# Low parts of the attention keys on both halves of the partitions, in a hybrid two-layer trunk

## The chip, the cores and the metric

The kernel runs on one core of a Trainium2 chip. The metric is the device time of one execution in microseconds (us), lower being better. Before the change the median of 3 runs is 1223.11 us (1218.67 to 1227.75). A difference of about 1% is what a measurement of this kernel can tell from no change.

The engines go by short names: PE is the matrix engine (PEld its weight loads, which overlap with matmuls), DVE the vector engine, ACT the scalar engine, POOL the GpSimd engine, and SP the queue that issues most loads from DRAM. Matmuls read their two operands from SBUF, a memory of 128 partitions, and write to PSUM, eight banks of 128 x 512 floats.

## What is computed

A decoder trunk of two layers on 512 tokens of 1024 columns, in float32. Layer 0 mixes with a sliding-window attention (mixer A: 8 heads over 2 key heads, window 128) and a forgetting attention (mixer B: 8 heads, each with its own keys). Layer 1 mixes with a sparse attention (mixer C: 8 heads over one key head, the 128 best keys of each query by an indexer of 4 heads) and a latent attention (mixer D: 8 heads). Each layer ends in a mixture of 16 experts, of which every token takes two. Cut to what matters here:

```python
logits = jnp.einsum('bqhd,bshd->bhqs', q_i, k, preferred_element_type=jnp.float32) * scale
logits = logits + c_i[..., :, None] - cum[:, :, None, :]          # mixer B
p = jax.nn.softmax(jnp.where(pos[None, :] <= t[:, None], logits, -jnp.inf), axis=-1)
dots = jnp.einsum('bqhe,bse->bqhs', qi_i, k_idx, preferred_element_type=jnp.float32) * IDX_DIM ** -0.5
score = jnp.einsum('bqh,bqhs->bqs', w_i, jax.nn.relu(dots))       # indexer of mixer C
_, idx = lax.top_k(score, top_k)
```

The head dimension is 64 in A, B, C and the indexer. Mixer D has 96 and isn't touched by the change.

## The kernel before, in words

**Numbers in two parts.** A value that enters an important matmul is split into a high part H with 12 significant bits and a low part L, the rest. A projection takes three matmuls (`mm3`, lines 196 to 199: H by H, H by L, L by H), each with 128 partitions of each operand. The splits stand in `unit` (line 176, weights: H by ACT on line 184, L by DVE or POOL on line 185) and `split_to` (line 201).

**Heads.** A projection gives two heads at once, one on partitions 0 to 63 and one on 64 to 127 (`HALF`, line 298). `stack_q` (line 305) makes for each head one tile of 128 partitions: the head's qH on its own half and its qL on the other. `stack_k` (line 313) makes for each key head a tile with kH on both halves (`dup`: ACT writes the head's own half on line 317, POOL copies it to the other half on line 303) and puts kL of both heads in one tile, each on its own half (`low`: DVE, line 319). Then `logits` (line 322) takes two matmuls into one PSUM bank:

```python
T.matmul(Sp, q, dup, start=True, stop=False)
T.matmul(Sp, q[HALF[h]], low[HALF[h]], start=False, stop=not more)
```

The first (line 324) has 128 rows and gives qH kH + qL kH; the second (line 325) has 64 rows, those of the head's own half, and adds qH kL.

**Where logits are called.** `attn_a` (line 710; 4 pairs of heads x 4 tiles of 128 queries x 2 heads = 32 calls, 128 or 256 keys wide), `attn_b` (line 748; 32 calls, 128 to 512 keys; a bf16 matmul that adds the mask follows, line 385), `index_scores` (line 915; 12 calls, 256 to 512 keys) and `attn_c` (line 1003; 32 calls, 128 to 512 keys). That makes 108 calls. A softmax follows, for two heads together (line 335): a maximum on DVE (line 344 where a bias is added, else line 348), an exponential on ACT (line 358), a division on DVE (line 366). Then come transposes on PE (line 374), a copy to SBUF on ACT (line 377) and the product with the values on PE (line 380, which writes 64 columns of the array at a time).

**Order of the work.** Instructions are issued in an order that a scheduler makes from the program's own order and its model of costs; it puts projections between the logits and the later steps of attention, so that PE has work while a softmax runs. The order of each engine is fixed when the program is built. The even mixer (layer 0, from line 618) runs the values, A's keys, then q and attention of A in turns, then k and q of B's first four heads (`k_b(0)`, `q_b(0)`), their attention, `k_b(1)`, `q_b(1)`, and their attention by tile of queries, with the output projection between (`EVEN_ORDER`). The odd mixer (from line 833) runs the latents, the keys `kc` of C and `ki` of the indexer (line 901 to 906), the indexer's scores, and then the parts named in `ODD_ORDER`: attention D beside `top_keys` (line 967, DVE: 16 rounds of maximum and replacement for each of three tiles), then attention C. `kc` and `ki` already have both H and L on both halves: lines 905 and 906 split both parts and copy both to the other half.

**Memory.** In the even mixer keys lie in two slots `ks0` and `ks1` of 6 x 512 floats a partition (`k_tiles`, line 640: four `dup` and two `low`). A's keys take ks0, `k_b(0)` ks1, `k_b(1)` ks0 again. The experts' pool `mo` lies over the mixer's memory once that is done: a place for the first loads of weights (`AHEAD`, line 42) is written when what the mixer kept there has been read. SP issues these loads in a fixed order.

Of the kernel before, what the change touches and what calls it, by code (L numbers as in the profile page):

```python
# [9 lines left out]
F32 = mybir.dt.float32  # L10
# [23 lines left out]
# slots of an expert for its tokens; with more than these, dense_moe  # L34
CAP = 96
OOB = 2048.0
# banks for products of long sums, of short ones, transposes and the branches' outputs
PS_A, PS_S, PS_T, PS_O = 2, 3, 2, 1
# loads of experts' weights in the ring of their own
RING = 5  # L40
# the loads that are issued while the mixer runs, in order: numbers in the order of their use
AHEAD = (2, 3, 4, 0, 1, 5, 6, 8, 9, 10, 12, 13, 7, 14, 11, 15)
# columns on DVE, the others on Pool and ScalarE: of the affine part of a layer's first LN, by tile; of the last step of
# its second. Columns on Pool: of that LN's centring
# [3 lines left out]
# units whose low parts Pool brings, not DVE: (matrix, expert) -> numbers  # L48
LOW_ON_POOL = {("d", 14): (3,), ("d", 15): (2,)}
# orders of the parts that may be moved against each other: what they are stands where they are run  # L50
# [15 lines left out]
def trunk_kernel(ctx: ExitStack, tc, x_in, even_w_in, even_b_f, even_sinks, odd_w_in,  # L66
# [12 lines left out]
    class Rows:  # L79
        """[8 * 128, S] in two tiles"""  # L80
# [20 lines left out]
    # key - query, in the last blocks of a row of keys  # L101
# [11 lines left out]
    # the activations' table, ahead of the first use  # L113
# [14 lines left out]
    # heads' slopes and their inverses are powers of two: 2^-(h+1)  # L128
# [5 lines left out]
    # slots, counted from one  # L134
# [7 lines left out]
    # tokens, less 2048  # L142
# [8 lines left out]
    def spread(dst, src):  # L151
        """a row to all partitions, which costs DRAM but one of them"""
        nc.gpsimd.dma_start(dst[0:1, :], src.unsqueeze(0))
        G.partition_broadcast(dst, dst[0:1, :], channels=128)
# [21 lines left out]
    def unit(w, eng=V):  # L176
        """w = H + L with 12 significant bits each; w: [128, a, b], at most 1024 elements"""
# [10 lines left out]
    def ksplit(w, n, eng=V):  # L188
        """units along k: list over k of (H, L) rows"""
# [15 lines left out]
    def rsqrt(var, eps, n, pin=lambda ins: ins):  # L205
        """1 / sqrt(var + eps): first bits from the exponent, then a step of third order and one of second"""
# [3 lines left out]
        def square(r, v):  # L210
            """r * r * v"""
# [13 lines left out]
        # q * (15 - 10 c + 3 c c) / 8 without its factor 3/8, which the last step brings  # L225
# [7 lines left out]
    def ln_stats(sts):  # L233
        """-> means and variances [128, n, 2], 1/sqrt(var + eps) [128, n]"""
        n = len(sts)
        mv = sm.tile([128, n, 2], F32, name="mv", tag=f"mv{n}")
        for j, st in enumerate(sts):
            V.bn_aggr(mv[:, j, :], st)
        return mv, rsqrt(mv[:, :, 1], LN_EPS, n)
# [10 lines left out]
    def affine(x, gb, bb, nv):  # L250
        """x * gb + bb, the last nv columns on DVE"""
# [5 lines left out]
    # residual stream, updated in place  # L257
    xr = [None] * NT

    def new_xr(j, nm="xr"):  # L260
        """room for two tiles of it"""
# [17 lines left out]
    def proj_t(w, XH, XL, eng=V):  # L279
        """[128 columns, tokens] = w^T x; w: raw view [128, 8, 128]"""  # L280
# [15 lines left out]
    # heads in pairs, on 64 partitions each; logits as [qH; qL] . [kH; kH] + qH . kL, a pair's other head with  # L296
    # qL above qH
# [7 lines left out]
    def stack_q(o, scales, dst):  # L305
        """o: a pair's queries [128, S] -> dst: one tile for each head"""
# [6 lines left out]
    def stack_k(o, dup, low):  # L313
        """o: keys of two heads [128, S] -> dup: [kH; kH] for each head, low: kL of both"""
        for h in range(2):
            a, b = HALF[h], HALF[1 - h]
            A.copy(dup[h][a], o[a])
            ins = copy_pool(dup[h][b], dup[h][a])
            V.tensor_tensor(out=low[a], in0=o[a], in1=dup[h][a].bitcast(F32), op=ALU.subtract)
        return ins  # L320

    def logits(Sp, h, q, dup, low, more=False):
        """q: [128, queries], dup and low: [128, keys]"""
        T.matmul(Sp, q, dup, start=True, stop=False)
        T.matmul(Sp, q[HALF[h]], low[HALF[h]], start=False, stop=not more)

    def pair(n, get):
        """two heads' [128, n], side by side in one tile where they fit, and what to copy to have both"""
# [6 lines left out]
    def softmax(work, Sp, n, bias=None, slopes=None, sink=None, norm=V):  # L335
        """two heads' logits in PSUM -> probabilities in SBUF. bias: a [128, n] tile for each head, or None.
        slopes: (list of two slopes, their negatives [128, 2]): the logits come divided by the slope.
        sink: (sinks over slopes [128, 2], sinks [128, 2])"""
# [44 lines left out]
    def causal(S_, nb):  # L383
        """adds the mask to the diagonal block, the last of nb"""
        T.matmul(S_[:, (nb - 1) * 128:nb * 128], idb, trib, start=False, stop=True)

# [8 lines left out]
    def router_fold(l):  # L395
        """the router on x1 = (y - mean) * rstd * g + b, from y and rstd alone: the weights times g, less their
        mean over the rows, and b's part"""
# [15 lines left out]
    def choose(t0, t1):  # L413
        """fills O and M for some tiles from aff: one-hot choices, their sum"""
# [5 lines left out]
        # the two best of four add up to the largest sum of a pair  # L420
# [9 lines left out]
        # the first of the best groups; the others sink  # L430
# [25 lines left out]
    def weights():  # L456
        """the choices' affinities over their sum"""
# [9 lines left out]
    def slots(sl, oh0, t0, t1):  # L467
        """slots of some tiles' tokens, counted from one: of each expert, 0 elsewhere; the first expert's one-hot"""
# [3 lines left out]
        # a tile's tokens come after those of all tiles before  # L472
# [930 lines left out]
```

## Time and profile before

| | |
|---|---|
| median of 3 runs | 1223.11 us |
| the runs | 1218.67, 1227.75, 1223.11 us |
| span of the profiled execution, first to last instruction | 1213.8 us |
| what lies around the span, against the median | 9.3 us |
| first matmul of the logits, A | 48 us |
| last logits of B | 203 us |
| first matmul of the experts, layer 0 | 284.8 us |
| indexer's logits | 646 to 663 us |
| logits of C | 755 to 828 us |
| mean granted clock of PE | 0.955 |

The profile gives no time of its own for the profiled execution beside its span; the runs' times are of other executions. How to read it: the view by stretches gives the busy time of each engine in a stretch, with the number of its instructions in brackets. A matmul's end is modelled and neighbours overlap, so a busy PE says that PE had something in flight, not that it ran at its peak. What a matmul really costs in a row of matmuls is the distance from its start to the next one's start, which the timeline shows. A form such as `64*128 64x256` is a matmul with 64 rows by 128 columns of weights, and 256 columns streamed past. The granted clock is the share of the full rate at which PE was let run.

### The profile page before, as it was taken

Reading aid. Unit: us, or ns where it says so; the run is one execution under the profiler, and the core shown is the slowest. Engines: PE = TensorE matmul, PEld = TensorE weight load, DVE = VectorE, ACT = ScalarE, POOL = GpSimd, SP = SyncE. Lnnn points to the kernel's source line nnn. Section 1 sums busy time; section 2 is a strip of 40 time slices with the busy share of each in tenths; the row PEclk is TensorE's granted clock in tenths of the full one; section 3 lists DMA queues with packets and bytes.
Section 4 is the critical chain, followed back from the end, with each engine's and each line's share of the span. In section 5 each row is a group of like instructions: output and inputs, shape, how many; then the busy total and the mean of one; then the engine's idle time right before and its main releaser. Section 6 shows DMA issues by size and latency. Waiting matters only on the chain. (4 is left out here: it accounts for less than half of the span.)

```text
span 1213.8 us, 16654 instructions
## 1 busy us (share of the span) xinstructions
PE 1128.6 (93%) x5739; PEld 823.3 (68%) x5739; DVE 939.1 (77%) x1866; ACT 763.0 (63%) x1229; POOL 263.4 (22%) x223
## 2 busy tenths in 40 slices
PE   6999999988999999998599999999889999999982
PEld 6786776876777777776377665677767777777761
DVE  3646546587999999996866999455879999999967
ACT  3447455234888888886335745444348888888862
POOL 2001230052111141103602234001421111411023
PEclk9999999998999999999699999699889999999986
DMA  8313423488999997997412211222789999979962
GB/s 203 114 35 67 92 53 140 165 315 298 309 344 354 346 342 252 362 368 244 136 27 70 70 35 63 77 105 93 263 315 302 341 354 350 333 250 359 376 209 111
DMA packets 139613, 262.25 MB, mean 216 GB/s; under 512 B 11831, under 2 KB 28247, under 8 KB 139520
## 3 DMA queue, kind: packets, MB, share of 16 engines
q1 hardware_dynamic: 129232, 234.62, 55.9%
q0 software_dynamic: 10288, 26.48, 8.8%
q8 instruction: 47, 0.77, 0.3%
q14 instruction: 46, 0.38, 0.1%
HBM read 246.73 MB, written 22.30 MB: 222 GB/s over the span
## 5 line engine op out<-in xcount | busy, mean ns | idle before, releaser
L185 DVE TENSOR_TENSOR wl<-wraw,wh 128x1024 fp32r<-128x1024 f32 (+1 forms) x418 | 504.3, 1232 | 83.6 <-ACT wh L184 73.8
L184 ACT CAST wh<-wraw 128x1024 fp32r<-128x1024 f32 (+3 forms) x436 | 445.4, 1038 | 149.0 <-PE ps_s L199 66.3
L197 PE MATMUL ps_s<-wh,m 128*96 128x512 f32 (+1 forms) x528 | 208.7, 395 | 1.7 <-ACT m L202 1.7
L198 PE MATMUL ps_s<-wl,m 128*96 128x512 f32 (+1 forms) x528 | 206.8, 392 | 0.0
L199 PE MATMUL ps_s<-wh,m 128*96 128x512 f32 (+1 forms) x528 | 205.2, 389 | 0.4 <-DVE m L203 0.4
L199 PEld LDWEIGHTS ps_s<-wh,m 128*96 128x96 f32 x528 | 86.7, 164 | 35.7 <-DVE m L203 1.3
L197 PEld LDWEIGHTS ps_s<-wh,m 128*96 128x96 f32 x528 | 86.9, 165 | 34.5 <-ACT m L202 2.1
L198 PEld LDWEIGHTS ps_s<-wl,m 128*96 128x96 f32 x528 | 86.7, 164 | 31.9
L198 PE MATMUL ps_a<-wl,hH 128*96 128x512 f32 x256 | 101.7, 397 | 5.6 <-POOL wl L185 5.6
L197 PE MATMUL ps_a<-wh,hH 128*96 128x512 f32 x256 | 102.8, 402 | 3.4 <-ACT hH L202 3.4
L199 PE MATMUL ps_a<-wh,hL 128*96 128x512 f32 x256 | 101.1, 395 | 1.3 <-DVE hL L203 1.3
L197 PE MATMUL ps_a<-wh,XH 128*128 128x512 f32 (+2 forms) x224 | 88.4, 395 | 2.4 <-ACT wh L184 1.3
L1096 POOL DMA_INDIRECT m<-x1d,idx x30 | 33.2, 1106 | 255.1 <-PE ps_t L1107 233.9
L199 PE MATMUL ps_a<-wh,XL 128*128 128x512 f32 (+2 forms) x224 | 87.7, 391 | 0.4 <-DVE XL L203 0.4
L1171 POOL DMA_INDIRECT yd<-m,idx x30 | 49.0, 1634 | 177.1 <-ACT m L1170 176.1
L198 PE MATMUL ps_a<-wl,XH 128*128 128x512 f32 (+2 forms) x224 | 86.8, 388 | 0.0
L377 ACT COPY pT<-ps_t 128x512 f32<-128x512 f32 (+2 forms) x88 | 43.7, 519 | 52.8 <-PE ps_t L374 49.7
L198 PE MATMUL ps_a<-XL,wh 128*128 128x512 f32 x160 | 65.9, 412 | 0.0
L197 PE MATMUL ps_a<-XH,wh 128*128 128x512 f32 x160 | 65.5, 410 | 0.0
L199 PE MATMUL ps_a<-XH,wl 128*128 128x512 f32 x160 | 65.1, 407 | 0.3 <-DVE wl L185 0.3
L358 ACT ACTIVATE p<-p,nm 128x256 f32<-128x256 f32 (+3 forms) x96 | 50.7, 530 | 19.4 <-DVE nm L351 11.6
L198 PEld LDWEIGHTS ps_a<-wl,hH 128*96 128x96 f32 x256 | 41.5, 162 | 22.1 <-POOL wl L185 7.0
(325 smaller groups left out, 1934.7 us busy)
## 6 DMA issues: line engine op xcount, KB each, us to landing
wraw<-in_moe_w_up_dram SPq DMA_DIRECT2D x64, 1024.0 KB, 11.6
wraw<-in_moe_w_gate_dram SPq DMA_DIRECT2D x64, 1024.0 KB, 12.0
wraw<-in_moe_w_down_dram SPq DMA_DIRECT2D x64, 1024.0 KB, 11.9
wraw<-in_w_o_dram SPq DMA_DIRECT2D x6, 1024.0 KB, 4.9
wraw<-in_even_w_in_dram SPq DMA_DIRECT2D x4, 1024.0 KB, 5.1
x1d<-xr POOLq DMA_DIRECT2D x8, 512.0 KB, 7.6
yd<-xr POOLq DMA_DIRECT2D x8, 512.0 KB, 9.3
xr<-yd SPq DMA_DIRECT2D x8, 512.0 KB, 5.1
```

What stands on the lines that cost most here:

```text
L184: first(A.copy(hv, w))
L185: first(eng.tensor_tensor(out=lv, in0=w, in1=hv.bitcast(F32), op=ALU.subtract))
L197: T.matmul(o, lh, rh, start=first, stop=False)
L198: T.matmul(o, lh, rl, start=False, stop=False)
L199: T.matmul(o, ll, rh, start=False, stop=last)
L358: A.activation(out=pt[h], in_=(pt if bias else Sp)[h], func=AF.Exp, bias=nm[:, h:h + 1], scale=(slopes[0][h] if slopes else 1.0), accum_ou ...
L377: A.copy(d_, s_)
L1096: G.indirect_dma_start(out=xg_of[e], out_offset=None, in_=x1d[:, :], in_offset=bass.IndirectOffsetOnAxis(ap=idx[:CAP, e:e + 1], axis=0), b ...
L1171: G.indirect_dma_start(out=yd[:, :], out_offset=bass.IndirectOffsetOnAxis(ap=idx[:CAP, e:e + 1], axis=0), in_=yos[e % 2], in_offset=None, ...
```

## The change

`stack_k` now uses `split_to` for both parts and copies both to the other half, so that kL stands on both halves as kH does; `logits` multiplies the whole q tile, 128 rows, with the low parts. The second matmul gives qH kL + qL kL, where before it gave qH kL alone. In the even mixer a pair of key heads has one tile of [128, 2 heads, 2 parts, 512] (8 KB a partition), and there are three slots of it, ks0 to ks2, in place of two slots of 12 KB: A's keys take ks0, `k_b(0)` ks1 and ks2, `k_b(1)` ks0 and ks1. A tile of 152 floats named "gap" is put ahead of `oht` in the experts' pool, which moves all that follows by 608 bytes. The calls hand over the new tiles. Comments are dropped, which the diff below leaves out.

```diff
-    def stack_k(o, dup, low):
+    def stack_k(o, dst):
         for h in range(2):
             a, b = HALF[h], HALF[1 - h]
-            A.copy(dup[h][a], o[a])
-            ins = copy_pool(dup[h][b], dup[h][a])
-            V.tensor_tensor(out=low[a], in0=o[a], in1=dup[h][a].bitcast(F32), op=ALU.subtract)
-        return ins
+            split_to(dst[h][a, 0, :], dst[h][a, 1, :], o[a])
+            copy_pool(dst[h][b], dst[h][a])
 
-    def logits(Sp, h, q, dup, low, more=False):
-        T.matmul(Sp, q, dup, start=True, stop=False)
-        T.matmul(Sp, q[HALF[h]], low[HALF[h]], start=False, stop=not more)
+    def logits(Sp, q, k, more=False):
+        T.matmul(Sp, q, k[:, 0, :], start=True, stop=False)
+        T.matmul(Sp, q, k[:, 1, :], start=False, stop=not more)
...
             work.tile([128, 4, CAP], F32R, name="hL", tag="hL")
+            work.tile([128, 152], F32, name="gap")
             oht = work.tile([CAP, S], F32R, name="oht")
...
-            def k_tiles(j):
-                return ev.tile([128, 6, S], F32R, name="ks", tag=f"ks{j}")
-            def k_split(t):
-                return t[:, 0:4, :], t[:, 4:6, :]
-            kb0 = k_tiles(1)
+            def k_pair(j):
+                return ev.tile([128, 2, 2, S], F32R, name="ks", tag=f"ks{j}")
+            kb0 = [k_pair(1), k_pair(2)]
...
-                dup, low = k_split(ks)
                 for b in range(2):
-                    stack_k(proj_t(W[:, :, b * 128:(b + 1) * 128], XH, XL), [dup[:, 2 * b + a, :] for a in range(2)],
-                            low[:, b, :])
-                return dup, low
+                    stack_k(proj_t(W[:, :, b * 128:(b + 1) * 128], XH, XL), [ks[b][:, a] for a in range(2)])
+                return ks
...
-                        logits(Sp[h], h, qs[:, 2 * (b % 2) + h, i * 128:(i + 1) * 128], ka[0][:, h, k0:k0 + n],
-                               ka[1][:, 0, k0:k0 + n])
+                        logits(Sp[h], qs[:, 2 * (b % 2) + h, i * 128:(i + 1) * 128], ka[:, h, :, k0:k0 + n])
...
-                        logits(Sp[h], h, qs[:, 2 * (b % 2) + h, i * 128:(i + 1) * 128],
-                               ks[0][:, 2 * (b % 2) + h, :n], ks[1][:, b % 2, :n], True)
+                        logits(Sp[h], qs[:, 2 * (b % 2) + h, i * 128:(i + 1) * 128], ks[b % 2][:, h, :, :n], True)
...
-            ka = k_split(k_tiles(0))
-            stack_k(proj_t(wload(cols(512, 128), 8, 128), XH, XL), [ka[0][:, a, :] for a in range(2)], ka[1][:, 0, :])
+            ka = k_pair(0)
+            stack_k(proj_t(wload(cols(512, 128), 8, 128), XH, XL), [ka[:, a] for a in range(2)])
...
-            ks, q1 = k_b(1, k_tiles(0)), q_b(1, q_tiles(1))
+            ks, q1 = k_b(1, [k_pair(0), k_pair(1)]), q_b(1, q_tiles(1))
...
-                        logits(Sp[h], h, qi[:, 2 * b + h, i * 128:(i + 1) * 128], ki[:, 0, :n], ki[:, 1, :n])
+                        logits(Sp[h], qi[:, 2 * b + h, i * 128:(i + 1) * 128], ki[:, :, :n])
...
-                        logits(Sp[h], h, qc[b // 2][:, 2 * (b % 2) + h, i * 128:(i + 1) * 128], kc[:, 0, :n], kc[:, 1, :n])
+                        logits(Sp[h], qc[b // 2][:, 2 * (b % 2) + h, i * 128:(i + 1) * 128], kc[:, :, :n])
```

## The prediction

> **What bounds the kernel now.** I first read the view by stretches, since a mean over the whole span hides that the stages differ (the columns: stretch, its length, busy us of PE with its instructions in brackets, of PEld, DVE, ACT, POOL; granted clock; DMA share, GB/s).
>
> ```profile
> 60.00:80.00 20.00, 20.00 (x119) 15.28 (x118) 10.76 (x43) 10.15 (x31) 0.00 (x0) 1.00 0.17 53
> 180.00:200.00 20.00, 18.91 (x105) 12.04 (x104) 14.89 (x54) 12.06 (x35) 2.40 (x1) 1.00 0.58 211
> 340.00:360.00 20.00, 20.00 (x98) 14.32 (x97) 18.43 (x18) 17.04 (x21) 2.58 (x2) 1.00 1.04 357
> 640.00:660.00 20.00, 19.83 (x89) 14.26 (x88) 11.47 (x38) 10.49 (x21) 6.25 (x5) 1.00 0.24 77
> 680.00:700.00 20.00, 19.94 (x114) 13.85 (x113) 19.15 (x57) 10.43 (x24) 5.75 (x9) 1.00 0.16 54
> 760.00:780.00 20.00, 20.00 (x72) 13.44 (x72) 8.20 (x45) 8.06 (x30) 0.06 (x1) 0.51 0.29 105
> ```
>
> In layer 0's attention (60 to 80) PE has something in flight all the time while DVE and ACT are busy half of it: PE bounds. The experts (340 to 360) are bound by PE too, with DMA near its limit. The indexer's logits (640 to 660) are bound by PE; behind them (680 to 700) DVE is full with the search for the best keys, and a shorter matmul buys nothing there. Attention C (760 to 780) is bound by PE again, at a granted clock of 0.51, with only 72 matmuls in 20 us.
>
> A busy PE isn't a PE at its peak, so next I looked at starts in PE's timeline: two calls of the logits with 128 keys, then one with 256, and beside them matmuls of a projection.
>
> ```profile
> 68.94 0.33 PE L324 MATMUL ps_s<-ks,qs 128*128 128x128 f32 x1
> 69.20 0.32 PE L325 MATMUL ps_s<-ks,qs 64*128 64x128 f32 x1
> 69.45 0.38 PE L324 MATMUL ps_s<-ks,qs 128*128 128x256 f32 x1
> 69.77 0.38 PE L325 MATMUL ps_s<-ks,qs 64*128 64x256 f32 x1
> 70.08 0.38 PE L324 MATMUL ps_s<-ks,qs 128*128 128x256 f32 x1
> 71.26 0.31 PE L197 MATMUL ps_a<-wh,XH 128*128 128x324 f32 x1
> 71.41 0.31 PE L198 MATMUL ps_a<-wl,XH 128*128 128x324 f32 x1
> ```
>
> From 69.45 to 69.77 to 70.08: a matmul of 256 columns holds PE for 0.32 us on either side of the 64-row one, while one of 324 columns among its like holds it for 0.15. The time isn't in the columns. Is it in the first matmul of the logits, or in the step to 64 rows? Where line 324 is followed by another instruction of 128 rows, it is short:
>
> ```profile
> 98.94 0.24 PE L324 MATMUL ps_s<-ks,qs 128*128 128x128 f32 x1
> 99.05 0.33 PE L374 MATMUL ps_t<-ident,p 128*128 128x128 f32 x1
> 99.31 0.32 PE L325 MATMUL ps_s<-ks,qs 64*128 64x128 f32 x1
> ```
>
> The same 128 columns held PE for 0.11 us ahead of the transpose, and for 0.26 ahead of line 325 (68.94 to 69.20); the transpose, 128 columns too, held it for 0.26 once line 325 came behind it. So each change between 128 and 64 rows costs about 0.15 to 0.2 us, twice a call. The changed kernel has none of these between its two matmuls.
>
> **The change part by part.** First the second matmul. How many, by width:
>
> ```profile
> L325 PE MATMUL ps_s<-ks,qs x64: 322/381/501, 48.4 to 202.5; 64*128 64x256 f32 x32, 64*128 64x128 f32 x16, 64*128 64x384 f32 x8, 64*128 64x512 f32 x8
> L325 PE MATMUL ps_s<-kc,qs x32: 323/482/580, 755.0 to 827.1; 64*128 64x128 f32 x8, 64*128 64x256 f32 x8, 64*128 64x384 f32 x8, 64*128 64x512 f32 x8
> L325 PE MATMUL ps_s<-ki,qs x12: 381/438/501, 646.8 to 662.9; 64*128 64x512 f32 x4, 64*128 64x384 f32 x4, 64*128 64x256 f32 x4
> ```
>
> The wide ones, with 128-row references:
>
> ```profile
> 645.55 0.33 PE L197 MATMUL ps_a<-wh,latq 128*128 128x384 f32 x1
> 645.72 0.34 PE L198 MATMUL ps_a<-wl,latq 128*128 128x384 f32 x1
> 652.29 0.49 PE L325 MATMUL ps_s<-ki,qs 64*128 64x512 f32 x1
> 652.71 0.45 PE L197 MATMUL ps_a<-wh,latq 128*128 128x384 f32 x1
> 655.49 0.44 PE L324 MATMUL ps_s<-ki,qs 128*128 128x384 f32 x1
> 655.86 0.44 PE L325 MATMUL ps_s<-ki,qs 64*128 64x384 f32 x1
> ```
> ```profile
> 177.05 0.39 PE L198 MATMUL ps_a<-XL,wh 128*128 128x512 f32 x1
> 177.28 0.40 PE L199 MATMUL ps_a<-XH,wl 128*128 128x512 f32 x1
> ```
> ```profile
> 766.88 0.58 PE L324 MATMUL ps_s<-kc,qs 128*128 128x256 f32 x1
> 767.39 0.58 PE L325 MATMUL ps_s<-kc,qs 64*128 64x256 f32 x1
> 779.23 0.63 PE L198 MATMUL ps_a<-wl,XH 128*128 128x512 f32 x1
> 779.66 0.63 PE L199 MATMUL ps_a<-wh,XL 128*128 128x512 f32 x1
> ```
>
> A call, now and then: 128 keys 0.26 + 0.25 = 0.51, then 2 x 0.11: 0.29 less. 256 keys 0.63, then 2 x 0.13 (between the 0.11 of 128 columns and the 0.15 of 324): 0.37 less. 384 keys 2 x 0.37 = 0.74, then 2 x 0.17: 0.40 less. 512 keys 2 x 0.42 = 0.84, then 2 x 0.23: 0.38 less. At half clock 256 keys take 2 x 0.51 = 1.02, then about 0.45 (512 columns take 0.43 there): 0.57 less. I assume that 64 rows more in the same columns cost nothing, as the 128-row references say.
>
> Layer 0: 16 x 0.29 + 32 x 0.37 + 8 x 0.40 + 8 x 0.38 = 22.7 us. Indexer: 4 x (0.37 + 0.40 + 0.38) = 4.6. Attention C: 8 x (0.29 + 0.57 + 0.40 + 0.38) = 13.1, with the 256 keys at half clock. Together 40.4 us. Not every neighbour is a 128-row one: the product with the values uses 64 columns, and next to it a switch stays.
>
> ```profile
> 100.20 0.28 PE L324 MATMUL ps_s<-ks,qs 128*128 128x256 f32 x1
> 100.41 0.44 PE L380 MATMUL ps_o<-pT,vt 128*64 128x128 f32 x4
> ```
>
> Here 256 columns of 128 rows hold PE for 0.21 us. By the timeline some 16 of the 216 sides of the second matmuls are such; I take 8% off: layer 0 20.9, indexer 4.2, C 12.1, in all 37 us of PE.
>
> How much of that reaches the end? In layer 0, PE already comes before the data in places:
>
> ```profile
> PEld ps_o L380 <- ACT pT L377: 4.2, 13, 0.4
> ```
>
> In 13 places between 44 and 250 us PE waits for the copy that ends a softmax, and its 32 steps of attention (16 in A, 16 in B) have such a place each. There, PE time saved turns into waiting, until the projections put between shift. I take 83% of layer 0's share: 17.3. The indexer feeds the stage where DVE is full; DVE starts earlier but already has other work: half, 2.1 (bounds 0 and 4.2). C has slack on DVE and ACT (8 of 20 us): 85%, 10.3. Sum 29.7 us. Bounds: nothing hidden, 37; half of layer 0 and C and nothing of the indexer, 16.5.
>
> Whether the gain of layer 0 survives the experts depends on their weights arriving as much earlier. SP's queue waits for places that the mixer frees:
>
> ```profile
> SPq L1088 <- PE ps_a L199: 42.1, 1, 42.1
> ```
>
> That wait ends on the output projection on PE, so the loads move with it. If DMA could not follow, the 17.3 would be lost, and 12.4 stay.
>
> Now the keys. DVE's and ACT's work is the same (10 each). POOL's ten copies get twice as long: 1.04 in place of 0.61 us, by the row of `kc`, which has both parts already.
>
> ```profile
> L303 POOL TENSOR_SCALAR ks<-ks x10: 613/616/1171, 38.7 to 173.7; 64x512 fp32r<-64x512 f32 x10
> L303 POOL TENSOR_SCALAR kc<-kc x1: 1045/1045/1045, 640.6 to 640.6; 64x1024 fp32r<-64x1024 f32 x1
> ```
> ```profile
> 173.00 1.31 POOL L303 TENSOR_SCALAR ks<-ks 64x512 fp32r<-64x512 f32 x2
> 176.25 2.40 POOL L185 TENSOR_TENSOR wl<-wraw,wh 128x1024 fp32r<-128x1024 f32 x1 [1.95 <-ACT wh L184]
> ```
> ```profile
> 180.31 0.22 PE L324 MATMUL ps_s<-ks,qs 128*128 128x128 f32 x1
> ```
>
> Each copy now also waits for DVE's low part (0.69 us). Behind the last pair wait only POOL's split of a weight (2.40) and the first logits of `k_b(1)`, which start at 180.31, 6.0 us after the copies end at 174.31; the queries are projected between. The copies get 4 x 0.43 = 1.7 longer and 0.7 later, and the cover holds: nothing on the path. Without it, 2.4 us. The other three pairs of copies stand ahead of query projections likewise.
>
> The slots: `k_b(1)` writes ks1 for its second pair, whose old keys are read last around 141 us and whose writes come at 170. `oht`, `oh0` and the first tiles of the router now lie where keys are read up to 203 us, but these are written behind the output projection. The experts' loads get places with no later last reader. All this I take at nothing; the bound is again the 17.3 us that are lost if the weights can't come earlier.
>
> **By the skill.** A rule speaks against the change: the Trainium skill, TensorE: Matmul & The Clock Gate, Part 3 (The mechanism), states that a weight load overlaps with matmuls in flight only when the row groups differ. By it, a second 128-row load would stand behind the first matmul, and the sum would be near nothing: 1223, rival 3 below. The trace disagrees: the 128-row matmuls at 177.05 and 177.28 each have a load of their own and still start 0.23 us apart. The measurement decides.
>
> **The rivals.**
> 1. *The clock comes back.* Attention C runs at 0.51 from 760 to 780, when logits with their switches make up most of PE's work; projections in layer 0 keep it at 1.00. With denser columns it may stay full: the 11 us of work that 20 us at half rate hold (0.23 to 0.43) then save up to 9 more, of which C's half-clock surplus (8 x 0.20) is counted. With a better share of the sum (33 + 7): 1183. Against: the stretch of 128 keys is short of columns even without switches. No row tells the cause of the 0.51. The Trainium skill, TensorE: Matmul & The Clock Gate, Part 1, states that about 3.4 us of sustained work bring the full clock back; no run here shows it yet.
> 2. *The softmax takes PE's place.* PE's order is fixed, so logits done earlier wait for the maximum, exponential and copy, whose lengths stay. For it: the 13 waits and 18.91 of 20 us at 180 to 200. Against: DVE and ACT are half idle. Half the gain: 16.5, 1207.
> 3. *It isn't the rows.* If the cost belongs to two short matmuls into one bank, or to a load that waits for the matmul ahead, 128 rows change nothing: 1223. Against: 98.94, and projections, which add into one bank at full pace.
> 4. *Slower: the clock drops in layer 0.* If PE waits a little in each softmax, the clock could fall to half there as in C. A stretch of 20 us at half loses 9 us; from the fourth on it outweighs the 29.7; five make 1223.1 - 29.7 + 46 = 1239. Against: 1.00 there now, and columns get denser.
>
> **How the numbers follow.** Forecast 0.52, clock 0.19, softmax 0.19, not the rows 0.06, slower 0.04. The sum goes against the profiled span of 1213.8 us: 1184.1 after, and with the 9.3 us around it to the median, 1193.4. Its own range is 1185 to 1202. Toward the clock's return and the softmax's 1207 with the runs' own spread of about 4 us either way I reach to 1179 and 1211; outside lie 2 in 10 at most. Faster by over 1% (below 1211; 1% is about what a measurement here tells from no change): forecast, clock and most of the softmax, 0.87. Within 1%: the rest of it, rival 3 and a part of 4: 0.10. Slower: 0.03.
>
> **What would show it.** Line 325's successor reads 128*128; a call of 256 keys spans about 0.26 us and not 0.63; PE's instructions stay 5739; the first expert starts some 17 us earlier than 284.8; a round of one expert is unchanged; POOL's ten copies take 1.04 us. The prediction is wrong if second matmuls keep 0.3 us between starts, if waits of PE for ACT in layer 0 grow beyond 10 us, or if the experts' first matmuls wait for weights.

## The result, and the profile after

Four runs of the changed kernel have a median of 1188.31 us (1181.30 to 1197.56), four of the one before 1223.71 us: a ratio of 0.9737, 95% interval 0.9689 to 0.9785. The forecast was 1193.4. The profiled execution is the slowest of the four: span 1195.7 us, time 1197.56, mean granted clock 0.957. Runs over 1.5% above the fastest run of their kernel are left out of every comparison below: three of ten of e3, the profiled one among them, and four of the kernel before.

First the view by stretches of the changed kernel (columns as in the prediction). The stages start some us earlier, so the stretches are those of the same work.

```profile
60.00:80.00 20.00, 19.89 (x137) 16.27 (x136) 11.33 (x47) 10.61 (x33) 0.00 (x0) 1.00 0.17 53
180.00:200.00 20.00, 20.00 (x146) 14.63 (x147) 15.34 (x62) 14.48 (x44) 0.00 (x0) 1.00 0.53 198
335.00:355.00 20.00, 20.00 (x95) 14.18 (x94) 18.45 (x20) 17.05 (x20) 2.56 (x2) 1.00 1.04 359
675.00:695.00 20.00, 19.94 (x117) 14.36 (x116) 18.88 (x56) 10.32 (x21) 5.62 (x9) 1.00 0.15 53
755.00:775.00 20.00, 19.80 (x150) 15.08 (x149) 15.73 (x71) 15.18 (x50) 0.41 (x1) 1.00 0.29 106
```

PE is as "busy" as before, but 20 us of layer 0 hold 137 matmuls in place of 119, and 20 us of attention C 150 in place of 72, at a clock of 1.00 where it was 0.51. The experts (335 to 355) and the search (675 to 695) look as they did. The profile's page counts the same 5739 matmuls as before. Two calls with 128 keys and two with 256 in PE's timeline:

```profile
67.74 0.28 PE L323 MATMUL ps_s<-ks,qs 128*128 128x128 f32 x1
67.86 0.27 PE L322 MATMUL ps_s<-ks,qs 128*128 128x128 f32 x1
67.97 0.28 PE L323 MATMUL ps_s<-ks,qs 128*128 128x128 f32 x1
68.08 0.33 PE L322 MATMUL ps_s<-ks,qs 128*128 128x256 f32 x1
68.25 0.28 PE L323 MATMUL ps_s<-ks,qs 128*128 128x256 f32 x1
68.47 0.39 PE L322 MATMUL ps_s<-ks,qs 128*128 128x256 f32 x1
68.69 0.28 PE L323 MATMUL ps_s<-ks,qs 128*128 128x256 f32 x1
68.81 0.31 PE L197 MATMUL ps_a<-wh,XH 128*128 128x324 f32 x1
```

Line 322 is now the first matmul of a call and 323 the second, both of 128*128. The call of 128 keys from 67.86 to 68.08 holds PE for 0.22 us (before 0.51, from 68.94 to 69.45), that of 256 keys from 68.47 to 68.81 for 0.34 (before 0.63).

How long the stages last is read from the first and last start of the second matmul:

```profile
L323 PE MATMUL ps_s<-ks,qs x64: 272/282/562, 49.6 to 192.9; 128*128 128x256 f32 x32, 128*128 128x128 f32 x16, 128*128 128x384 f32 x8, 128*128 128x512 f32 x8
L323 PE MATMUL ps_s<-kc,qs x32: 273/309/505, 750.3 to 806.5; 128*128 128x128 f32 x8, 128*128 128x256 f32 x8, 128*128 128x384 f32 x8, 128*128 128x512 f32 x8
L323 PE MATMUL ps_s<-ki,qs x12: 278/336/401, 642.4 to 655.9; 128*128 128x512 f32 x4, 128*128 128x384 f32 x4, 128*128 128x256 f32 x4
```

Layer 0's attention: 154.1 us before (48.4 to 202.5), 143.3 now, 10.8 less. Attention C: 72.1 before, 56.2 now, 15.9 less. The indexer's logits take 2.6 us less (16.1, now 13.5), but from their last to the first of C it is 94.4 us where it was 92.1: 2.3 of the 2.6 are given back to the search on DVE.

The first logits themselves came 1.2 us later in this execution (48.4, now 49.6). The first expert's first matmul has 8.6 us to show (284.8 before), and nothing in brackets that it waited for:

```profile
276.19 0.77 PE L197 MATMUL ps_s<-wh,m 128*96 128x512 f32 x1
```

Then the waits in layer 0's attention (44 to 204; us in total, times, longest), the changed kernel first and below it the rows of the kernel before:

```profile
PE ps_s L322 <- DVE mx L342: 3.0, 3, 2.4
PE ps_s L322 <- DVE qs L310: 1.8, 2, 1.2
...
PEld ps_s L322 <- DVE mx L342: 5.7, 8, 2.7
PEld ps_o L378 <- ACT pT L375: 4.8, 15, 0.4
...
PEld ps_s L323 <- issue: 0.3, 2, 0.2
```
```profile
PE ps_s L324 <- DVE qs L310: 1.1, 1, 1.1
...
PEld ps_s L325 <- issue: 8.4, 39, 0.4
PEld ps_o L380 <- ACT pT L377: 3.1, 10, 0.4
```

The queue of weight loads stood idle 39 times ahead of the second matmul's load for no reason that the profile names; this row is all but gone (0.3 in 2 places). A new one has come: the next call's first matmul waits for DVE's maximum of an earlier call (line 342), which frees its bank, for 3.0 us on PE where there was no such wait.

### The profile page after: what moved, and what is told of

It is laid out like the page before. It is cut to its first block, busy times and chain, and to the rows that moved or that the text cites. A ratio compares the mean times of both kernels' runs of the same rounds, so it can differ in the third digit from the quotient of the medians.

```text
span 1195.7 us, 16655 instructions
## 1 busy us (share of the span) xinstructions
PE 1098.3 (92%) x5739; PEld 816.4 (68%) x5739; DVE 935.3 (78%) x1866; ACT 763.3 (64%) x1229; POOL 263.2 (22%) x223
## 4 chain that ended last, share of the span: by engine, by line
PE 80%; DVE 10%; ACT 5%; issue 2%; POOL 2%; DMA 1%; SPq 0%; DVEq 0%; ACTq 0%; POOLq 0%
PE ps_a L198 11%; PE ps_a L199 11%; PE ps_a L197 11%; PE ps_s L197 10%; PE ps_s L198 10%; PE ps_s L199 9%; PE ps_o L378 4%; PE ps_t L372 3%; DVE wl L185 2%; ACT wh L184 2%; PE ps_t L1100 2%; PE ps_s L322 1%; POOL wl L185 1%; PE ps_s L323 1%; PE ps_s L578 1%
## 5 line engine op out<-in xcount | busy, mean ns | idle before, releaser
L375 ACT COPY pT<-ps_t 128x512 f32<-128x512 f32 (+2 forms) x88 | 43.6, 518 | 31.8 <-PE ps_t L372 28.3
```

The source lines that it names most:

```text
L375: A.copy(d_, s_)
```

## The experiments

**How times are compared.** The runs of one kernel spread over 10 to 15 us, and most of that goes with the clock. Within each kernel, over 113 runs of all kernels, time falls by 10.1 us for each 0.01 of mean granted clock (what is left has a standard deviation of 2.4 us). 0.01 of 1200 us is 24 us at half rate, so a us at half rate costs 0.42 us. So beside each median I give the mean moved along this slope to a clock of 0.960; for 4 runs it is good to about 1.2 us, for the 47 of the kernel before that ran beside the experiments to 0.4.

```
kernel                        runs  median   mean clock  at 0.960
before                          47  1218.1   0.9566      1214.5
changed, first runs              4  1188.3   0.9622      1191.1
e5  changed, again               4  1188.9   0.9625      1191.5
e1  128 rows in indexer and C    9  1206.9   0.9592      1205.4
e2  128 rows in layer 0          4  1201.2   0.9595      1200.6
e3  new tiles, 64 rows           7  1214.8   0.9587      1213.4
e4  before, heads grouped       10  1210.1   0.9603      1211.5
e6  before, 64 rows twice        4  1258.9   0.9372      1236.2
e7  changed, 128 rows twice     10  1206.3   0.9611      1208.1
e9  changed, 96 rows             4  1190.6   0.9620      1192.1
e11 changed, POOL divides in A   4  1193.2   0.9608      1193.8
e12 the same in A, B and C       4  1199.3   0.9595      1198.6
```

**One part of the change alone.** e1 takes the kernel before and gives 128 rows to the indexer and attention C, where the low keys already lie on both halves; e2 takes the changed kernel and goes back to 64 rows there; e3 goes back everywhere and keeps the new tiles, slots and copies.

```diff
 e1 (from before)
-    def logits(Sp, h, q, dup, low, more=False):
+    def logits(Sp, h, q, dup, low, more=False, rows=None):
-        T.matmul(Sp, q[HALF[h]], low[HALF[h]], start=False, stop=not more)
+        r = rows or HALF[h]
+        T.matmul(Sp, q[r], low[r], start=False, stop=not more)
 calls with ki and kc: + rows=slice(0, 128)
 e2, e3 (from the changed kernel)
-    def logits(Sp, q, k, more=False):
+    def logits(Sp, q, k, more=False, r=slice(0, 128)):
-        T.matmul(Sp, q, k[:, 1, :], start=False, stop=not more)
+        T.matmul(Sp, q[r], k[r, 1, :], start=False, stop=not more)
 calls with ki and kc (e2), with ki, kc, ka and ks (e3): + r=HALF[h]
```

e1: 

> The kernel before, with 128 rows in the second matmul of the indexer and of attention C alone; layer 0 is as before. If the switch between 128 and 64 rows is the cost: from the indexer's first logits to C's last the two profiles stand at 181.0 us before and 164.8 changed, so 16 us less, part of it from the clock in C: 1223.7 - 16 = 1208 us (1203 to 1213), layer 0 unchanged, and the stretch at half clock in C gone or shorter. If the new tiles, slots and copies of layer 0 bring the gain: no change, 1223 us.

e2: 

> The changed kernel, with 64 rows again in the indexer and in attention C. If the rows are the cost: layer 0's share alone, between the 8.6 us that the first expert's start moved in the profiles and the 17 us that were predicted, so 1207 to 1215 us, and the half clock in C is there as before. If C's gain hangs on the timing that layer 0 hands on: the half clock in C is gone here too, and the time is below 1205.

e3: 

> The changed kernel's tiles, slots, gap and doubled copies on POOL, with 64 rows in every second matmul. It adds only copies to the kernel before. If the rows are the cost: as before, 1223 us (1219 to 1228). If the placement of tiles or the copies matter: near the changed kernel's 1188 if they bring the gain, or above 1230 if they cost.

Against the kernel before on the same chip (median 1217.96): e1 0.9915 (0.9882 to 0.9947), e2 0.9884 (0.9832 to 0.9935), e3 0.9971 (0.9932 to 1.0009). The tiles and copies alone bring nothing (e3's range was counted from the 1223 of the first runs; on its own chip before and e3 are the same within the error). At equal clock the indexer and C bring 9.1 us and layer 0 13.9, 23.0 together; the changed kernel has 23.2. The parts add up, and of the changes made it is the rows that bring the time.

e1 fell within its range. e2 did not: 1201.2 lies below the 1207 to 1215 of its first theory, C has 64 rows there and no stretch at half clock, and that is what its second theory said. But C's gain is not handed on by layer 0: with 64 rows and the full clock e2's C takes 63.7 us, 8.4 less than in the profile of before, where the changed kernel's takes 56.2. Only the half clock is missing, and by e8 below the kernel before itself doesn't have it in C in every execution. C in e2:

```profile
L323 PE MATMUL ps_s<-kc,qs x32: 322/410/502, 745.6 to 809.3; 64*128 64x128 f32 x8, 64*128 64x256 f32 x8, 64*128 64x384 f32 x8, 64*128 64x512 f32 x8
```

**Fewer changes of rows, same rows.** e4 issues both heads' 128-row matmuls, then both heads' 64-row ones.

```diff
-        T.matmul(Sp, q, dup, start=True, stop=False)
-        T.matmul(Sp, q[HALF[h]], low[HALF[h]], start=False, stop=not more)
+        for h, (q, dup, low) in enumerate(args):
+            T.matmul(Sp[h], q, dup, start=True, stop=False)
+        for h, (q, dup, low) in enumerate(args):
+            T.matmul(Sp[h], q[HALF[h]], low[HALF[h]], start=False, stop=not more)
```

> The kernel before, with the two heads' 128-row matmuls one after the other, and then their two 64-row matmuls, one on the upper and one on the lower half of the rows. If each change of the row count costs 0.15 to 0.2 us: two changes for two heads in place of four, so about half of the sum, some 15 to 18 us of PE and 10 to 18 us of time: 1206 to 1214 us. If the cost is that two short matmuls into one bank follow each other: no such neighbours are left, and the time is near 1188. If a weight load waits for the matmul ahead: every second matmul keeps its 0.3 us, 1223 us.

0.9953 (0.9916 to 0.9989): within the first theory's range by the median, but at equal clock only 3.0 us. The trace says why it tells little: other stages' matmuls are put between the calls, and in 13 of the 54 pairs only do the two 64-row matmuls follow each other. There they start 3 to 4 ns apart: on different halves they run side by side. The Trainium skill, TensorE: Matmul & The Clock Gate, Part 3 (The mechanism), states just this for tiles on different rows.

**The disputed cost by itself.** e6 issues the 64-row matmul of the kernel before twice, e7 the second 128-row one of the changed kernel; the low product is then added twice. e5 is the changed kernel again, on the same chip.

```diff
 e6 (from before)
+        T.matmul(Sp, q[HALF[h]], low[HALF[h]], start=False, stop=False)
         T.matmul(Sp, q[HALF[h]], low[HALF[h]], start=False, stop=not more)
 e7 (from the changed kernel)
+        T.matmul(Sp, q, k[:, 1, :], start=False, stop=False)
         T.matmul(Sp, q, k[:, 1, :], start=False, stop=not more)
```

e5: 

> The changed kernel as it is, beside the one before and the next two on one chip. Over the runs so far, time falls by 11.1 us for each 0.01 of mean granted clock, and at an equal clock of 0.960 the changed kernel stands 23 us below the one before (1191.4 against 1214.4); the layer 0 part (13.8) and the part in the indexer and C (9.0) add up to it. Theory, rows bring 23 us and a higher clock the rest: again 23 +-2 at equal clock, and a ratio of 0.973 to 0.983 by how the clock falls. Rival, the two parts do not add up and the 23 was chance of few runs: outside 19 to 27 at equal clock. Whether C has a stretch at half clock is open: none if rows alone keep it away, in some profiles only if its place against the other windows decides.

e6: 

> The kernel before with the 64-row matmul of each call issued twice in succession, so that the low product is added twice: 108 matmuls more, and not one change of rows more. Theory, the price is in the change between 128 and 64 rows: the second of the pair costs what a matmul among its like does, 0.06 us (128 keys), 0.12, 0.17 and 0.23 (512), 14.7 us in all on PE, of which 62% arrive as they did for the change itself (23 of 37): 9 us more than before at equal clock, 5 to 15. Rival, a 64-row matmul, or a second one into the same bank, costs 0.25 to 0.42 us by itself: 35 us on PE, 22 more in time, 18 to 36.

e7: 

> The changed kernel with the 128-row matmul of the low parts issued twice in succession, the low product added twice: 108 matmuls more. Theory: like its counterpart with 64 rows, 14.7 us on PE, 9 us more than the changed kernel at equal clock, 5 to 15; the same start distances as there, since rows in themselves cost nothing. Rival, 128 rows cost more than 64 where no row change is in play: over 4 us more than the counterpart adds.

e5: 0.9789 (0.9697 to 0.9881), 23 us at equal clock, as expected. e7: 0.9917 (0.9880 to 0.9953), 16.6 us above the changed kernel at equal clock: PE's added 16 us arrive in full and not to 62%. My range ended at 15, so that share does not carry over from work removed to work added. e6: 1.0352 (1.0243 to 1.0461), 40 us; 21.7 at equal clock, the rest a mean clock of 0.937. In time that is above the theory's 5 to 15. Its timeline, PE and then the loads:

```profile
73.22 0.38 PE L324 MATMUL ps_s<-ks,qs 128*128 128x256 f32 x1
73.54 0.39 PE L325 MATMUL ps_s<-ks,qs 64*128 64x256 f32 x1
73.77 0.28 PE L326 MATMUL ps_s<-ks,qs 64*128 64x256 f32 x1
73.97 0.39 PE L324 MATMUL ps_s<-ks,qs 128*128 128x256 f32 x1
```
```profile
73.22 0.19 PEld L324 LDWEIGHTS ps_s<-ks,qs 128*128 128x128 f32 x1
73.54 0.18 PEld L325 LDWEIGHTS ps_s<-ks,qs 64*128 64x128 f32 x1
73.65 0.19 PEld L326 LDWEIGHTS ps_s<-ks,qs 64*128 64x128 f32 x1
73.97 0.19 PEld L324 LDWEIGHTS ps_s<-ks,qs 128*128 128x128 f32 x1
```

From 73.54 to 73.77 no rows change, and yet the 64-row matmul of 256 columns holds PE for 0.23 us where a 128-row one can hold it for 0.12 (68.69 to 68.81 above). The loads say why. At a change of rows the load stands at the very start of its own matmul (73.54, 73.97), not ahead of it, and it is this matmul, line 325's, that holds PE longer. The load of line 326 does run ahead: it starts 0.11 us into the matmul before it (73.65), 0.12 before its own. A 128-row matmul whose load doesn't run ahead is as slow. In the changed kernel the load at 68.47 starts with its matmul, which then holds PE for 0.22 us; the load at 52.69 is 0.17 us ahead, and its matmul holds PE for 0.12:

```profile
68.47 0.19 PEld L322 LDWEIGHTS ps_s<-ks,qs 128*128 128x128 f32 x1
68.58 0.19 PEld L323 LDWEIGHTS ps_s<-ks,qs 128*128 128x128 f32 x1
```
```profile
52.69 0.19 PEld L322 LDWEIGHTS ps_s<-ks,qs 128*128 128x128 f32 x1
52.86 0.19 PEld L323 LDWEIGHTS ps_s<-ks,qs 128*128 128x128 f32 x1
```
```profile
52.86 0.28 PE L322 MATMUL ps_s<-ks,qs 128*128 128x256 f32 x1
52.98 0.28 PE L323 MATMUL ps_s<-ks,qs 128*128 128x256 f32 x1
```

So the neighbours of a call at the same width are sorted by whether the first one's own load ran ahead (traces of before, after, e6, e7 and e9 at full clock; us from start to start, medians of 2 to 89 cases):

```
own load 0.1 us or more ahead of its matmul
columns   128->128   128->96   128->64   64->128
128       0.060      0.059     0.152     -
256       0.118      0.118     0.209     0.206
384       0.174      0.176     0.268     0.265
512       0.232      0.231     0.327     0.323
own load within 5 ns of its matmul's start
columns   128->128   128->96   128->64   64->128   64->64, same half
128       0.163      0.165     0.257     0.254     0.164
256       0.223      0.223     0.315     0.313     0.223
384       0.282      0.282     0.372     0.369     0.280
512       0.336      0.337     0.425     0.426     0.338
```

Two prices come out of it, each the same at every width. A change of rows costs about 0.09 us, down or up (0.209 or 0.206 against 0.118; 0.315 or 0.313 against 0.223). A load that starts only with its own matmul costs 0.10 to 0.11 us more, with 128, 96 or 64 rows alike (0.223 against 0.118). The two come together: behind a change of rows the load starts within 2 ns of its matmul in all 208 such pairs of logits, and between two 64-row matmuls on the same half it starts 0.056 us or more ahead in all 76. So 64-row matmuls on one half are no slower in themselves; the expectation of e9 below, which gives them 0.104 us, mistakes the late load of the first for a price of the second.

On PE the theory of e6 therefore holds. The second 64-row matmuls hold PE for 26 us in all, and 10 of them come back, since the load of the matmul ahead of the step up is no longer late (0.206 and not 0.313 at 256 columns). The 16 us that stay are what e7 adds, and near the theory's 14.7; the rival's 35 are not there. That e6 stands 21.7 higher at equal clock leans on a long way along the slope, from 0.937. The rule of the Trainium skill that the prediction set against the trace (TensorE: Matmul & The Clock Gate, Part 3 (The mechanism): a load overlaps only where row groups differ) does not hold here for 64 rows either: the load of line 326 starts 0.12 us ahead of its matmul, while line 325's on the same half is in flight.

**Fewer rows than 128, but more than 64.**

```diff
-        T.matmul(Sp, q, k[:, 1, :], start=False, stop=not more)
+        T.matmul(Sp, q[0:96], k[0:96, 1, :], start=False, stop=not more)
```

> The changed kernel with rows 0 to 95 alone in the second matmul (it leaves out the products of rows 96 to 127, so a part of the low terms). The doubled 64-row matmul showed that even with no change of rows between them one 64-row matmul starts 0.104 us later behind another than a 128-row one does (0.163 against 0.059 us at 128 columns, 0.335 against 0.232 at 512). Theory 1, this belongs to the step down to a half of the rows: the experts' matmuls with 96 rows follow 128-row ones at full pace in every profile, so 96 rows cost as 128 do, start distances 0.116 us at 256 columns, and 1191.5 +-2 at a clock of 0.960, the changed kernel's time. Theory 2, any matmul of fewer than 128 rows pays: distances as with 64 rows, 0.2 to 0.31 us, and 1210 to 1215 at that clock, the time of before.

0.9755 (0.9709 to 0.9802), 1192.1 at equal clock: theory 1. In its timeline 96 rows follow 128 at full pace, from 68.02 to 68.14 in 0.12:

```profile
67.40 0.33 PE L322 MATMUL ps_s<-ks,qs 128*128 128x256 f32 x1
67.57 0.28 PE L323 MATMUL ps_s<-ks,qs 96*128 96x256 f32 x1
67.80 0.39 PE L322 MATMUL ps_s<-ks,qs 128*128 128x256 f32 x1
68.02 0.28 PE L323 MATMUL ps_s<-ks,qs 96*128 96x256 f32 x1
68.14 0.31 PE L197 MATMUL ps_a<-wh,XH 128*128 128x324 f32 x1
```

In e9 101 of the 108 loads of the second matmul run ahead, as many as in the changed kernel, and in the kernel before none of 108 does. So it is not that rows are missing, but that 64 rows are a step that 96 are not.

**The clock, twice more.** e8 and e10 are the kernel before, unchanged.

e8: 

> The kernel before, unchanged, for a second profile of the clock. If half clock in attention C belongs to the kernel before, the stretch of 20.5 us that began 5.5 us after the first logits of C stands there again. If it depends on where C falls against the windows of 3.41 us at whose edges all half-rate stretches begin, it may be gone, and the span is then some 8 us below that of the first profile for equal clock elsewhere.

e10: 

> The kernel before, unchanged, for a third profile of the clock. The first had 20.5 us at half clock in attention C and none in layer 0's attention, the second 13.7 us in attention B and none in C. Theory: with 64-row matmuls some stretch of attention falls to half clock in each execution, 10 us or more in A, B and C together, and its place varies; the changed kernel's two profiles had 3.4 us each. Rival: the clock in attention is a matter of chance with either kernel, and 0 to 4 us is as likely here.

Stretches of e8, and its C; then the same of e10:

```profile
185.00:205.00 20.00, 18.93 (x76) 11.30 (x76) 10.33 (x43) 7.16 (x25) 0.07 (x1) 0.66 0.59 211
755.00:775.00 20.00, 19.80 (x124) 12.89 (x121) 16.22 (x63) 10.81 (x36) 3.44 (x6) 1.00 0.31 110
775.00:795.00 20.00, 20.00 (x115) 13.63 (x114) 13.36 (x44) 12.07 (x32) 0.00 (x0) 1.00 0.13 49
```
```profile
L325 PE MATMUL ps_s<-kc,qs x32: 322/408/501, 762.2 to 825.9; 64*128 64x128 f32 x8, 64*128 64x256 f32 x8, 64*128 64x384 f32 x8, 64*128 64x512 f32 x8
```
```profile
775.00:795.00 20.00, 20.00 (x97) 12.55 (x96) 10.37 (x41) 9.90 (x30) 0.00 (x0) 0.76 0.12 47
```
```profile
L325 PE MATMUL ps_s<-kc,qs x32: 322/439/580, 762.0 to 830.0; 64*128 64x128 f32 x8, 64*128 64x256 f32 x8, 64*128 64x384 f32 x8, 64*128 64x512 f32 x8
```

In e8 C has the full clock and takes 63.7 us; attention B loses it instead (0.66 from 185 to 205, 13.7 us at half rate). In e10 10.2 us of C are at half rate, and it takes 68.0. With 72.1 us at 20.5 in the first profile these lie on a line: 63.7 plus 0.41 us for each us at half rate. The half clock does not belong to C; it comes somewhere in attention, and where differs from one execution to the next. In A, B and C together the profiles show 20.5, 13.7 and 10.2 us at half rate for the kernel before, about 61 for e6 and none for e4; 0 and 3.4 for e1 and e2; 3.4 for both of the changed kernel, 3.4 to 6.8 for e7, e9, e11 and e12. The theory of e10 holds for the kernel before, but not for 64 rows as such: e4 has all 108 of them and no half rate in attention, in one profile. That more 64-row matmuls can bring the clock down is shown by e6 against e7: the same 108 matmuls added, clock 0.937 with 64 rows and 0.961 with 128. By what rule the clock is granted stays open.

**What took PE's place in layer 0.** e11 moves the division of the softmax in attention A from DVE to POOL, e12 that of A, B and C.

```diff
 e11; e12 does the same at the calls of attention B and C
-                                 (sinks[:, b:b + 5:4], sink[:, b:b + 5:4]))
+                                 (sinks[:, b:b + 5:4], sink[:, b:b + 5:4]), norm=G)
```

e11: 

> The changed kernel with the normalization of attention A (32 instructions of 128x128 and 128x256) on POOL in place of DVE. Layer 0's attention got 10.8 us shorter in the profile where its fewer exposed weight loads are worth 17.5, and PE there waits for DVE as it did not before (first matmul of the logits behind DVE's maximum: none, now 3.0 us in 3 places on PE). Theory, DVE's queue in layer 0 took the place of PE: freed of 32 x 0.3 us the waits for the maximum in A shrink and A, 54.95 us from its first logits to its last, gets 1 to 3 us shorter; time 1188 to 1191 at a clock of 0.960, 0 to 3 below the changed kernel. Rival, the chain of one softmax and not DVE's queue sets the pace: POOL's 0.1 us more per instruction makes A the same or up to 3 us longer.

e12: 

> The changed kernel with the normalization of attentions A, B and C on POOL (96 instructions, 33 us of DVE's time). Theory of the late DVE: 2 to 6 us below the changed kernel at equal clock (1185 to 1189 at 0.960), if POOL's splits of weights (2.4 us) and key copies do not get in its way. Rival, the chain sets the pace, or POOL's queue delays a normalization: 1192 to 1200.

e11 0.9802 (0.9746 to 0.9858), 2.5 us above the changed kernel at equal clock; e12 0.9864 (0.9803 to 0.9924), 7.3 above. The rival holds. e11's waits between 44 and 204:

```profile
PEld ps_t L372 <- POOL p L364: 6.6, 12, 3.0
...
PE ps_t L372 <- POOL p L364: 3.3, 2, 2.8
...
PE ps_s L322 <- DVE mx L342: 0.5, 2, 0.3
```

The wait for DVE's maximum shrank as the theory said, from 3.0 to 0.5 us, but the transposes now wait 3.3 us on PE for the division, and layer 0's attention takes 147.1 us in place of 143.3. POOL had been idle for 17 us before the instruction behind the longest of these waits (2.8 us), so in e11 it isn't POOL's queue that PE waits for but the softmax as a chain; an engine relieved at the price of a longer step buys nothing here. Some 1.4 of the 3.8 us are the clock, 6.8 us at half rate and not 3.4. In e12 the chain and POOL's queue are not told apart. No version of these beats the changed kernel.

## Why the prediction came out right, and where it was wrong

**The total is right, its make-up is not.** Forecast: 29.7 us, all of it from the rows. Measured over all runs: 1218.1 to about 1188.6, 29.5 us, of which 23.2 remain at equal clock; the other 6.3 come with a mean clock of 0.962 in place of 0.9566. The rows' term was a quarter too high, and the clock, which stood among the rivals, filled the gap. That the two agree to 0.2 us is luck. The 9.3 us that the prediction puts around the span do not lie around it: in every run with both on record the time is 1.8 to 2.2 us above the span, so most of the 9.3 says that the profiled execution was a faster one than the median.

**The price of a call: mis-sized.** The prediction's 0.15 to 0.2 us for a change of rows is right in size: 0.09 for the change and 0.10 to 0.11 for the load that can't run ahead. The step that failed is the other side of the subtraction, the "2 x 0.13" for 256 keys: it takes for granted that every load runs ahead once no rows change. In layer 0's attention the changes of rows went from 127 to 0, but of 866 matmuls 120 still have a load that starts only with them while PE has work (213 before): next to the product with the values and its 64 columns, in the mask's matmul, and where an instruction waits for another engine. The load at 68.47 is of the last kind: it starts 0.06 us behind the end of DVE's maximum of an earlier call, and so the rows 68.25, 68.47 and 68.69 are 0.22 us apart.

```profile
68.33 0.08 DVE L342 DVE_READ_ACCUMULATOR2_ANT mx<- 128x1 f32 x1
```

A reference from the same place, not from projections, would have shown it. By the table a call of 256 keys costs (0.209 + 0.313) - (0.118 + 0.118) = 0.29 us more with 64 rows, not 0.37; 128 keys 0.24 (with 0.110 from the second matmul to the next call's first), not 0.29; 384 and 512 keys 0.29, not 0.40 and 0.38. With the same counts: layer 0 17.5 (forecast 22.7, and 20.9 with its 8% off), indexer 3.5 (4.6, 4.2), C 8.8 at full clock (13.1, 12.1), 29.8 in all in place of 40.4 and 37. The traces say the same without a price. From the first matmul of layer 0's first call to that of its last one the same 866 matmuls take 10.8 us less, PE stands idle 5.8 us where it was 1.1, and 3.4 us at half rate cost 1.4: 16.9 us less of PE. In the indexer that is 2.6 + 0.8 = 3.4, in C, against e8 at full clock, 7.5 + 0.5 = 8.0; 28.3 in all.

**How much arrives: right in C, too much in layer 0 and the indexer.** C keeps 63.7 (e8) - 56.2 = 7.5 of 8.8, 85% (forecast 85%). The indexer keeps 0.3 of 3.5 (forecast half): DVE's search has no use for an earlier start. Layer 0 keeps 10.8 of 17.5 by the profile, 62% (forecast 83%, a share that it sets beside 13 waits and doesn't work out), 13.9 by e2 at equal clock. Most of the rest went into PE's own waits, 4.7 us more than before, and the clock's 1.4. The stages sum to 18.6, the runs say 23.2; the 4.6 between them I could not locate, since the experts' stretches differ by as much from one profile to the next.

**Nothing for the keys: right.** e3 stands 1.1 us below before at equal clock, within the error. POOL's copies are the 1.04 us of the forecast:

```profile
L303 POOL TENSOR_SCALAR ks<-ks x10: 1037/1043/1047, 41.4 to 169.3; 64x1024 fp32r<-64x1024 f32 x10
```

**What would show it.** Right: the successor of line 325 reads 128*128, 5739 matmuls on PE, the copies, no expert that waits for weights at its first matmul, successive experts 17.66 us apart in both traces, PE's waits for ACT in layer 0 at 4.8 us and not above 10. Wrong in size: a call of 256 keys is 0.34 us in the rows above and not 0.26, the first expert comes 8.6 us earlier and not 17.

**The rivals.** The clock's return (1) came in part, but not as described: it isn't C's own stretch, which the kernel before has in some executions and not in others. The softmax (2) took a part in layer 0: waits for the maximum 3.0 us that were not there, and e11 shows that it is the chain. That it is not the rows (3) fell, by e2 and e3. Its weight load that waits is there all the same and is half of the price; a change of rows brings it about, and so do other things that stay (120 of 866 matmuls above). The drop of the clock in layer 0 (4) came as one stretch of 3.4 us, about 1.4 us of time (0.83 from 95 to 105), with no weight beside the rest.

## What to carry to other kernels

A matmul on half of the rows between full ones costs 0.24 to 0.29 us more here, whatever its width, and up to 0.1 more in the matmul behind it, whose load can't run ahead: where the other half can hold anything that may be added (zeros, or as here a second product that belongs to the sum), fill it. Price a step from the start distances of the same instructions with and without it, and cost only what differs; a neighbour from another stage hides what both have. Read each matmul's weight load beside it: whether the load ran ahead decides 0.1 us. Where the granted clock varies from run to run, compare times at equal clock, or a gain of 2% is read off a spread of 1%.

## What was not expected of the hardware

- 96 rows behind 128 cost nothing (0.118 us at 256 columns), 64 rows cost 0.09 us going down and 0.09 coming back, each with a load that can't run ahead (0.10 to 0.11). The Trainium skill, TensorEngine Tiling (Array Packing), Key Properties, states that a change of tiling mode drains the engine. The 0.09 fits that; no run here tells a drain from another cause.
- The time from a matmul's start to the next one's depends on its own load: 0.118 us at 256 columns where the load ran 0.1 us ahead, 0.223 where it started with the matmul, for 64, 96 and 128 rows alike. Two 64-row matmuls on different halves start 3 to 4 ns apart.
- PE can be busy without a gap, by the profile and its modelled ends, and still lose half its clock, in e6:

```profile
203.00:223.00 20.00, 20.00 (x68) 10.97 (x69) 7.95 (x36) 6.36 (x21) 0.00 (x0) 0.50 0.47 176
```

  It ran 30.7 us like that from 202.6 on. The stretches at half rate in attention are whole multiples of 3.41 us in all these traces. The Trainium skill, TensorE: Matmul & The Clock Gate, Part 1, ties the half clock to idle windows of about that length; the length agrees, the idleness does not by this row. What exactly is counted stays open.
- The changed kernel's 23 us at equal clock came from 28 to 30 us of PE, while e7's added 16 us of PE cost 16.6: here work taken away ran into the next wait, and work added did not.
